# Last two experts' rows gathered, summed, normed and scattered; final norm of all rows moved behind expert 13

## The chip, the core and the metric

The kernel runs on one core of one Trainium2 chip. The time is that of one execution on the device, in microseconds (us). The engines are named as in the profile: PE does the matrix products, PEld loads their weights, DVE and ACT work on rows of elements and read the products' banks, POOL works on rows in SBUF only and issues the indirect transfers, SP issues the plain transfers.

## The reference, cut to what matters

One layer: norm and modulation, a mixer of two kinds of heads, then a mixture of 16 experts in which each expert chooses 128 of the 1,024 rows, and a last norm over every row. Only the end matters here:

```python
aff = softmax(einsum('bnd,de->bne', u, router_w))
gate, idx = lax.top_k(swapaxes(aff, 1, 2), 128)        # 128 rows for each expert
xs = u[idx]                                            # rows gathered
h = silu(xs @ w_gate) * (xs @ w_up)                    # 128 x 1024 by 1024 x 1024, per expert
y = (h @ w_down) * gate[..., None]
x = x + g2 * zeros(1024, 1024).at[idx].add(y)          # a row can be chosen by several experts
return x * rsqrt(mean(x * x, -1) + eps) * final_norm_w # all 1,024 rows
```

## The kernel before, in words

Everything up to the router's choice of rows is left alone by the change. It leaves in device memory `d_v` (the rows that experts read) and `d_acc` (the residual rows, 1,024 x 1,024, to which experts add), and in SBUF `idx` and `gate`, one column of 128 entries for each expert.

The loop over experts (L1330) then takes 16 turns. In turn e PE forms the gate product and the up product of expert e and the down product of expert e - 1 (`prod`, `down`), each of 8 weight tiles of 128 x 1,024. A weight tile is loaded by SP (`raw_load`), split by ACT into a rounded part and by DVE into the remainder (`split_w`, L922 and L923, DVE subtracting one SBUF tile from another), and multiplied in three passes of two products each. Four pairs of buffers hold split tiles; some 30 raw tiles in the list `free` let SP load far ahead, a freed tile being loaded again at once. `split_t` turns the rows of an expert by PE and splits them (`mh`, `ml` for the down product). After `down(e - 1)` POOL issues `scatter(e - 1)`: an indirect transfer that adds the 128 rows of `y` to `d_acc`. All engines take their instructions in the order of their own queue; the framework's scheduler writes that order, so a statement's place in the text is not its place in a queue.

The last two experts are not scattered. In turn 15 the kernel loads the last norm's weight (`fwb`), and builds one-hot matrices `ohs` (L1355) for the rows of experts 14 and 15. Behind the loop it loads all of `d_acc` as eight tiles of 128 rows (L1370), splits `y` of expert 14 and of expert 15 (L1373 and L1374, L1395 and L1396), and `rows_of` (L1383) multiplies the one-hot matrices by these, so that the rows of both experts arrive in a product bank in their places. `added` (L1406, L1407) adds them to the tile and takes the sum of squares; then come the root (L1414, and L1415 on POOL), the weight (L1418 on POOL, L1421 on DVE) and the scale (L1420 on ACT), and SP stores the tile (L1422). This chain of eight tiles starts when expert 15's down product (L1393) is done.

```python
        V.scalar_tensor_tensor(y[:, cs], po, gate[:, 15:16], g2b[j], op0=OP.mult, op1=OP.mult)
```

is the line (L1394) that yields half of expert 15's rows.

Of the kernel before, what the change touches and what calls it, by code (L numbers as in the profile page):

```python
# [9 lines left out]
F32 = mybir.dt.float32  # L10
# [9 lines left out]
P = 128  # L20
EPS = 1e-6
# [11 lines left out]
def tile_hybrid_block(ctx, tc, x, c, cx, c_ctx, ada_w, ada_b, norm1_w, w_in, conv_w, conv_b,  # L33
# [28 lines left out]
    def bank(tag, shape=(P, 512)):  # L62
        return psum.tile(list(shape), F32, name=tag, tag=tag, bufs={"mm": 4, "hg": 2, "ms": 2}[tag])
# [670 lines left out]
    srw, sorts = [tkr[:, 768:896], tkr[:, 896:1024], tk.tile([P, P], F32, name="srw")], []  # L734
    pos = const.tile([P, 8, 32], F32, name="lm", tag="lm", bufs=1)
    pay = tk.tile([P, 8, 16, 5], BF16, name="pay")
    last = tk.tile([P, 2], F32, name="last")
    slot = tk.tile([P, P], F32, name="slot")
    G.iota(slot, pattern=[[1, P]], base=-999, channel_multiplier=0, allow_small_or_imprecise_dtypes=True)
    same, low, other = (tk.tile([P, P], BF16, name=n) for n in ("same", "low", "other"))  # L740
# [166 lines left out]

    def take_r():

        raw = next(r for r in free if id(r) in tags)  # L910
        free.remove(raw)
        return tb(tags[id(raw)], [1024], 1, F32R)

    pairs = []

    def split_w():

        raw, (wh, wl) = raws.pop(0), pairs[0]
        pairs.append(pairs.pop(0))
        for i, r in enumerate(raw):  # L920
            cs = slice(1024 // len(raw) * i, 1024 // len(raw) * (i + 1))
            S.copy(wh[:, cs], r)  # L922
            V.tensor_sub(wl[:, cs], r, wh[:, cs])  # L923
        free.append(raw)
        raw_load()
        return wh, wl

    part = flat = lambda t: t.rearrange("p a b -> p (a b)")
# [325 lines left out]
    def pick(e):  # L1254

        oh = blk.tile([P, 8, P], BF16, name="mkt", tag="mkt", bufs=2)
        with tc.issue_after(found[-1].ins):
            V.tensor_tensor(oh, slot.unsqueeze(1).to_broadcast([P, 8, P]), pos[:, :, e:e + 1].to_broadcast([P, 8, P]), op=OP.is_equal)
        ps = bank("ms")
        for t in range(8):  # L1260
            T.matmul(ps[:, 0:5], oh[:, t, :], pay[:, t, e, :], start=(t == 0), stop=(t == 7))
        got = tb("got", [5], 2)
        S.copy(got, ps[:, 0:5])
        found.append(V.tensor_add(idx[:, e:e + 1], got[:, 3:4], got[:, 4:5]))
        if e > 13:
# [63 lines left out]
    gather(1)  # L1329
    for e in range(16):  # L1330
        pg, pu = [bank("mm"), bank("mm")], [bank("mm"), bank("mm")]
        prod(xh, xl, pg)
        if e < 14:
            pick(e + 2)
        prod(xh, xl, pu)
        if e == 0:
            hh, hl = (tb(n, [8, P], 1, F32R) for n in ("mh", "ml"))
            hb, y = (part(tb("go", [8, P], 2)) for _ in range(2))
            for j in range(2):
                g2b.append(part(tl("hsum", [4, P], 2)))  # L1340
                load(g2b[j], bass.AP(tensor=d_g.tensor, offset=d_g[3].offset + 512 * j, ap=[[0, P], [1, 512]]))
        if e < 15:
            split_t(xg, xh, xl)
        if e < 14:
            gather(e + 2)
        if e == 15:
            fwb = take(2)
            for j in range(2):
                load(fwb[j], bass.AP(tensor=final_w.tensor, offset=final_w.offset + 512 * j, ap=[[0, P], [1, 512]]))
            toks = take(2)[0]  # L1350
            G.iota(toks, pattern=[[1, 512]], base=0, channel_multiplier=0, allow_small_or_imprecise_dtypes=True)
            ohs = [take_r() for _ in range(2)]
            for i in range(2):
                for h in range(2):
                    V.tensor_scalar(ohs[i][:, 512 * h:512 * h + 512], toks, last[:, i:i + 1], -512.0 * h, op0=OP.subtract, op1=OP.is_equal)  # L1355
# [15 lines left out]
    ys = [[part(tb(n, [8, P], 1, F32R)) for n in ("xT", "mix")]]
    ys += [[[r[:, 512 * j:512 * j + 512] for j in range(2)] for r in (take_r(), take_r())]]
    S.copy(ys[0][0], y)  # L1373
    G.tensor_sub(ys[0][1], y, ys[0][0])  # L1374
    sq = tb("sq", [2, 8])
    sums = {}

    def rows_of(j, t):

        sums[j, t] = pb = bank("ms" if j else "mm")  # L1380
        for i in range(4):
            r = ys[i // 2][i % 2]
            T.matmul(pb, ohs[i // 2][:, t * P:(t + 1) * P], r[j] if i > 1 else r[:, 512 * j:512 * j + 512], start=(i == 0), stop=(i == 3))  # L1383

    for j in range(2):
        cs = slice(512 * j, 512 * j + 512)
        po = bank("hg")
        for q in range(4):
            wh, wl = weight()
            for k in (2 * q, 2 * q + 1):  # L1390
                fs_ = slice(512 * (k % 2), 512 * (k % 2) + 512)
                for p_, (l, r) in enumerate(((hh, wh), (hl, wh), (hh, wl))):
                    T.matmul(po, l[:, k, :], r[:, fs_], start=(k == 0 and p_ == 0), stop=(k == 7 and p_ == 2))  # L1393
        V.scalar_tensor_tensor(y[:, cs], po, gate[:, 15:16], g2b[j], op0=OP.mult, op1=OP.mult)  # L1394
        S.copy(ys[1][0][j], y[:, cs])  # L1395
        V.tensor_sub(ys[1][1][j], y[:, cs], ys[1][0][j])  # L1396
        if j == 0:
            for t in range(4):
                rows_of(0, t)
    def added(t):  # L1400
        if t > 3:
            rows_of(0, t)
        rows_of(1, t)
        for j in range(2):
            a = accs[t][:, 512 * j:512 * j + 512]
            V.tensor_add(a, a, sums[j, t])  # L1406
            S.activation(hb[:, 512 * j:512 * j + 512], a, AF.Square, scale=1.0 / 32, accum_out=sq[:, j, t:t + 1])  # L1407

    for t in range(9):
        if t < 8:  # L1410
            added(t)
        if t:
            a, r = accs[t - 1], tb("fr", [1], 4)
            V.tensor_scalar(r, sq[:, 0, t - 1:t], sq[:, 1, t - 1:t], EPS, op0=OP.add, op1=OP.add)  # L1414
            pw = G.tensor_tensor(r, r, mhalf[:, :1], op=OP.pow)  # L1415
        if t < 8:
            with tc.issue_after(pw.ins) if t > 5 else ExitStack():
                G.tensor_mul(accs[t][:, 0:512], accs[t][:, 0:512], fwb[0])  # L1418
        if t:
            S.mul(a[:, 0:512], a[:, 0:512], r)  # L1420
            V.scalar_tensor_tensor(a[:, 512:], a[:, 512:], r, fwb[1], op0=OP.mult, op1=OP.mult)  # L1421
            load(out[(t - 1) * P:t * P], a)  # L1422
# [27 lines left out]
```

## Time and profile before

| | us |
|---|---|
| three runs, median (lowest, highest) | 1563.09 (1559.11, 1565.22) |
| the profiled execution's own time | 1559.33 |
| its span in the trace | 1557.6 |

Times in the trace run from the start of the span. Of the 1.7 us between the profiled execution's time and its span the trace shows nothing. PE's clock was granted in full in most of the span; the mean is 0.967.

### The profile page before, as it was taken

The numbers are of one execution on the slowest core, as the hardware profiler recorded it, in microseconds if no ns is written. First come the engines' busy times: TensorE is split into PE (matmuls) and PEld (weight loads), VectorE is DVE, ScalarE is ACT, GpSimd is POOL, SyncE is SP. The second block draws the span as 40 slices with busy tenths as digits, with TensorE's granted clock in tenths as the row PEclk, the third lists the DMA queues.
The fourth block names the chain that finished last, engine by engine and source line by source line (L and its number), as shares of the span: only waits on it lengthen the run. The fifth ranks groups of instructions, "written<-read, shape, count | busy, mean of one in ns | idle before, by whom it ended". The sixth has DMA issues, their size and how long they took to land.

```text
span 1557.6 us, 23134 instructions
## 1 busy us (share of the span) xinstructions
PE 1447.8 (93%) x8121; PEld 1206.9 (77%) x8121; DVE 1230.4 (79%) x2193; ACT 864.7 (56%) x1454; POOL 174.8 (11%) x136
## 2 busy tenths in 40 slices
PE   7999999999999998988888947999999999999996
PEld 2899878888898896977677735888888888888764
DVE  3685577888866859546757796999999999998887
ACT  3764424334434343345545315777787787777775
POOL 0000000000002221210222110010000000000003
PEclk9999999999999998989898977999999999999998
DMA  9741311220334254276753486999999999999942
GB/s 268 258 128 31 110 54 35 75 82 22 115 102 142 82 149 149 72 194 211 223 183 112 158 320 211 370 391 374 386 387 384 385 389 383 387 376 362 352 141 109
DMA packets 181201, 337.31 MB, mean 217 GB/s; under 512 B 13560, under 2 KB 108348, under 8 KB 181084
## 3 DMA queue, kind: packets, MB, share of 16 engines
q1 hardware_dynamic: 176472, 319.99, 58.0%
q0 software_dynamic: 4320, 15.73, 4.1%
q8 instruction: 64, 1.05, 0.3%
q14 instruction: 53, 0.43, 0.1%
q10 hardware_dynamic: 292, 0.10, 0.0%
HBM read 303.38 MB, written 32.39 MB: 216 GB/s over the span
## 4 chain that ended last, share of the span: by engine, by line
PE 64%; DVE 13%; DMA 10%; issue 6%; ACT 4%; POOL 2%; SPq 0%; ACTq 0%; POOLq 0%; DVEq 0%
PE mm L1303 22%; PE mm L278 11%; PE hg L1303 10%; PE mm L286 5%; PE hg L350 3%; DMA MB<-d_nm 3%; DVE cacc L827 3%; PE hg L215 2%; PE ms L1288 2%; DMA wraw<-in_w_in_dram 1%; PE mm L1026 1%; PE ms L382 1%; POOL cacc L825 1%; DMA wraw<-in_ada_w_dram 1%; PE mm L496 1%
## 5 line engine op out<-in xcount | busy, mean ns | idle before, releaser
L286 PE MATMUL mm<-whi,uh 128*128 128x256 f32 (+1 forms) x512 | 145.6, 284 | 3.0 <-DVE Sb L386 1.3
L286 PE MATMUL mm<-wlo,uh 128*128 128x256 f32 (+1 forms) x512 | 145.1, 283 | 0.0
L286 PE MATMUL mm<-whi,ul 128*128 128x256 f32 (+1 forms) x512 | 144.8, 283 | 0.0
L253 DVE TENSOR_TENSOR wlo<-wraw,whi 128x512 fp32r<-128x512 f32 x96 | 64.7, 686 | 49.5 <-ACT whi L252 49.0
L286 PEld LDWEIGHTS mm<-whi,uh 128*128 128x128 f32 x512 | 96.7, 189 | 5.2 <-DVE Sb L386 1.5
L286 PEld LDWEIGHTS mm<-whi,ul 128*128 128x128 f32 x512 | 96.8, 189 | 0.0
L286 PEld LDWEIGHTS mm<-wlo,uh 128*128 128x128 f32 x512 | 96.3, 188 | 0.3
L1303 PE MATMUL mm<-qkx,xT 128*128 128x512 f32 x256 | 83.7, 408 | 0.6 <-ACT xT L1289 0.3
L827 DVE SCALAR_TENSOR_TENSOR cacc<-pad,cols,cacc 128x1024 f32<-128x1024 f32 x48 | 63.6, 1325 | 24.4 <-POOL cacc L825 23.6
L1303 PE MATMUL mm<-E,xT 128*128 128x512 f32 x256 | 81.2, 398 | 0.4 <-ACT E L922 0.4
L1303 PE MATMUL mm<-MB,xT 128*128 128x512 f32 x256 | 80.8, 397 | 0.0
L252 ACT CAST whi<-wraw 128x512 fp32r<-128x512 f32 x96 | 58.4, 620 | 38.3 <-PE mm L278 24.8
L344 ACT COPY hgc<-hgK 128x512 f32<-128x512 f32 x56 | 35.5, 634 | 78.1 <-DVE hgK L363 38.6
L350 PE MATMUL hg<-hgQ,hgc 128*128 128x128 f32 x448 | 65.9, 291 | 1.0 <-DVE hgQ L366 1.0
L350 PEld LDWEIGHTS hg<-hgQ,hgc 128*128 128x128 f32 x448 | 57.8, 191 | 10.8 <-issue 6.9
L278 PE MATMUL mm<-uh,whi 128*128 128x512 f32 x192 | 63.4, 405 | 0.0
L278 PE MATMUL mm<-ul,whi 128*128 128x512 f32 x192 | 63.4, 404 | 0.0
L278 PE MATMUL mm<-uh,wlo 128*128 128x512 f32 x192 | 61.5, 399 | 0.0
L297 DVE SCALAR_TENSOR_TENSOR ac<-wraw,csil,ac 128x256 f32<-128x256 f32 x112 | 55.9, 499 | 4.1 <-DMA wraw<-in_ada_w_dram 2.2
L1303 PEld LDWEIGHTS mm<-E,xT 128*128 128x128 f32 x256 | 47.9, 189 | 13.7 <-ACT E L922 1.7
L1303 PEld LDWEIGHTS mm<-MB,xT 128*128 128x128 f32 x256 | 48.2, 188 | 11.9
L359 DVE COPY_PREDICATED hgA<-lm,hg 128x512 f32<-128x512 uint8 x56 | 41.4, 740 | 18.4 <-PE hg L350 17.1
(602 smaller groups left out, 4304.2 us busy)
## 6 DMA issues: line engine op xcount, KB each, us to landing
wraw<-in_w_in_dram SPq DMA_DIRECT2D x48, 512.0 KB
wl<-in_exp_w_up_dram SPq DMA_DIRECT2D x34, 512.0 KB
wh<-in_exp_w_up_dram SPq DMA_DIRECT2D x34, 512.0 KB
wh<-in_exp_w_gate_dram SPq DMA_DIRECT2D x34, 512.0 KB
wl<-in_exp_w_gate_dram SPq DMA_DIRECT2D x34, 512.0 KB
wraw<-in_ada_w_dram SPq DMA_DIRECT2D x32, 512.0 KB
wl<-in_exp_w_down_dram SPq DMA_DIRECT2D x29, 512.0 KB
wh<-in_exp_w_down_dram SPq DMA_DIRECT2D x29, 512.0 KB
```

The lines of the kernel that those rows point to most:

```text
L215: T.matmul(pm[0:2, :256], csil[:, k, :], adas[i, k // 4][:, k % 4, :, :], start=(k == 0), stop=(k == 7))
L252: S.copy(hi[:, :, cs], src)
L253: V.tensor_sub(lo[:, :, cs], src, hi[:, :, cs])
L278: T.matmul(o, l, r[:, k, i * n:(i + 1) * n], start=(k == 0 and q == 0), stop=(k == 7 and q == 2))
L286: T.matmul(o, l[:, k, ts], r, start=(k == 0 and q == 0), stop=(k == 7 and q == 2))
L297: V.scalar_tensor_tensor(ac, a2[:, k % 4, :], csil[:, k, 0:1], ac, op0=OP.mult, op1=OP.add)
L344: S.copy(view(kc, 0, [[h, 2], [2 * h, 256 // h], [1, h]]), view(K, 0, [[512 + h, 2], [2 * h, 256 // h], [1, h]]))
L350: T.matmul(pb[:, cc, :], kc[:, cc * P:(cc + 1) * P], view(Q, cc * P, pat), start=True, stop=True)
L359: V.copy_predicated(A, lmask[h].unsqueeze(1).to_broadcast([P, 4, P]), scores(h))
L827: V.scalar_tensor_tensor(acc, tap(t), tapw(t, r), acc, op0=OP.mult, op1=OP.add)
L1288: T.transpose(pt[:, k, :], view(src, 4 * q + k, [[8, P]]), ident)
L1303: T.matmul(o, l[:, k, :], r[:, 512 * j:512 * j + 512], start=(k == 0 and p_ == 0), stop=(k == 7 and p_ == 2))
```

## The change

With e the turn: in turn 14, right after `scatter(13)`, `norm_start` asks for a first tile of `d_acc`, a gather of expert 14's 128 rows of `d_acc` into `rows_[14]`, the norm's weight as one 128 x 1,024 tile and a second tile of `d_acc`. From there `weight` advances the generator `norms` at every third call. Each step norms one tile of 128 rows as if no expert were still to come: the sum of squares on ACT, then on POOL a product with the weight, a sum, a power and a product with the root, and a store by SP two steps later. Thus all 1,024 rows are normed and stored without experts 14 and 15.

`row_out` then repairs the 256 rows of these two: DVE adds `y` to the gathered rows, ACT squares, POOL takes the root, DVE forms the normed rows, and POOL scatters them over `out`. Rows of expert 14 are also scattered back to `d_acc`, from which expert 15's rows are then gathered, since a row can belong to both. A scatter over `out` waits for every store before it (`add_manual_dep`). So that tiles are free for all this, ten freed raw tiles are not loaded again (`hold`). The one-hot matrices, their products, the splits of `y` and the chain behind expert 15 go.

```diff
@@ split_w
         free.append(raw)
-        raw_load()
+        if hold and len(raw) == 1:
+            hold.pop()
+        else:
+            raw_load()
@@ weight
+        if accs:
+            fin["n"] = fin.get("n", 0) + 1
+            if fin["n"] > 3 and fin["n"] % 3 == 1:
+                next(dense, None)
@@ new functions
+    def acc_rows(e):
+        rows_[e] = take(1)
+        G.indirect_dma_start(out=rows_[e], out_offset=None, in_=d_acc,
+                             in_offset=bass.IndirectOffsetOnAxis(ap=idx[:, e:e + 1], axis=0))
+    def norms():
+        for t in range(10):
+            if t > 1:
+                stored.append(load(out[(t - 2) * P:(t - 1) * P], accs[t - 2]))
+            if t + 2 < 8:
+                acc_load(t + 2)
+            if t < 8:
+                a, r = accs[t], sq[:, t:t + 1]
+                S.activation(fin["junk"], a, AF.Square, scale=1.0 / 32, accum_out=r)
+                G.tensor_mul(a, a, fin["w"])
+                G.tensor_scalar(r, r, EPS, None, op0=OP.add)
+                G.tensor_tensor(r, r, mhalf[:, :1], op=OP.pow)
+                G.tensor_mul(a, a, r.to_broadcast([P, 1024]))
+            yield
+    def row_out(e, js):
...
+            V.tensor_add(rows_[e][:, cs], rows_[e][:, cs], y[:, cs])
+            S.activation(y[:, cs], rows_[e][:, cs], AF.Square, scale=1.0 / 32, accum_out=sq[:, 8 + 2 * i + j:9 + 2 * i + j])
...
+        if e == 14:
+            G.indirect_dma_start(out=d_acc, out_offset=..., in_=rows_[14], in_offset=None)
+        r, o = tb("fr", [1], 2), hb if e == 15 else fin["junk"]
+        V.tensor_scalar(r, ..., EPS, op0=OP.add, op1=OP.add)
+        G.tensor_tensor(r, r, mhalf[:, :1], op=OP.pow)
+        V.scalar_tensor_tensor(o, rows_[e], r, fin["w"], op0=OP.mult, op1=OP.mult)
+        d = G.indirect_dma_start(out=out, out_offset=..., in_=o, in_offset=None)
+        for s_ in stored:
+            tc.add_manual_dep(d.ins, s_.ins.name, DATA, reason="rows stored again")
+        stored.append(d)
@@ the loop over experts
+        if e == 14:
+            hold.extend(range(10))
...
-        if e == 15:
-            fwb = take(2)
...
-                    V.tensor_scalar(ohs[i][:, 512 * h:512 * h + 512], toks, last[:, i:i + 1], -512.0 * h, ...)
...
+        if e == 14:
+            norm_start()
+        if e == 15:
+            for _ in dense:
+                pass
+            row_out(14, (0, 1))
+            acc_rows(15)
@@ behind the loop
-    accs = []
-    for i in range(8):
-        accs.append(take(1))
-        load(accs[i], d_acc[P * i:P * i + P])
...
-            T.matmul(pb, ohs[i // 2][:, t * P:(t + 1) * P], ...)
...
         V.scalar_tensor_tensor(y[:, cs], po, gate[:, 15:16], g2b[j], op0=OP.mult, op1=OP.mult)
-        S.copy(ys[1][0][j], y[:, cs])
-        V.tensor_sub(ys[1][1][j], y[:, cs], ys[1][0][j])
...
+        row_out(15, (j,))
```

What the scheduler makes of it shows in the queues. ACT, from the middle of expert 14's down product (L922 before, L921 now, is the split of a weight tile; the second cast of `mh` must wait until that down product has used up the first contents). Before:

```order
L922 CAST qkx<-xm 128x1024
L1289 CAST mh<-ms 128x512
L922 CAST E<-S_8976 128x1024
L922 CAST MB<-kin 128x512 x2
L922 CAST v_8613<-tkr 128x1024
L922 CAST qkx<-v_7887 128x1024
L1289 CAST mh<-ms 128x512
```

Now (L1355 is a norm's sum of squares):

```order
L921 CAST qkx<-xm 128x1024
L1289 CAST mh<-ms 128x512
L1355 ACTIVATE v_8346,sq<-S_8976 128x1024
L1355 ACTIVATE v_8346,sq<-wor 128x1024
L921 CAST E<-kin 128x512 x2
L921 CAST MB<-wor 128x1024
L921 CAST v_8612<-wor 128x1024
L1355 ACTIVATE v_8346,sq<-v_7416 128x1024
L1289 CAST mh<-ms 128x512
```

The first two squares stand between the first cast of `mh` and the casts of the last three weight tiles of expert 14's down product; no norm stands further ahead.

POOL, from the scatter of expert 13 on. Before, a few instructions between that scatter and the chain behind expert 15:

```order
L1314 DMA d_acc<-go,idx 1024x1024 x2
L1351 IOTA wh_8751 128x512
L1374 TENSOR_TENSOR mix<-go,xT 128x1024
L1418 TENSOR_TENSOR wl_8754<-wl_8754,Sb 128x512
L1418 TENSOR_TENSOR wh_8755<-wh_8755,Sb 128x512
```

Now (`S_8976`, `wor` and so on are the tiles of `d_acc`, L1356 the product with the weight, L1357 the sum with eps, L1358 the power, L1359 the product with the root):

```order
L1318 DMA d_acc<-go,idx 1024x1024 x2
L1333 DMA tkr<-d_acc,idx 128x1024
L1357 TENSOR_SCALAR sq<-sq 128x1
L1358 TENSOR_TENSOR sq<-sq,mhalf 128x1
L1356 TENSOR_TENSOR S_8976<-S_8976,v_7886 128x1024
L1359 TENSOR_TENSOR S_8976<-S_8976,sq 128x1024
L1356 TENSOR_TENSOR wor<-wor,v_7886 128x1024
L1357 TENSOR_SCALAR sq<-sq 128x1
L1358 TENSOR_TENSOR sq<-sq,mhalf 128x1
L1359 TENSOR_TENSOR wor<-wor,sq 128x1024
```

All eight tiles run through POOL with four instructions each.

POOL's end, before and then now:

```order
L1415 TENSOR_TENSOR fr<-fr,mhalf 128x1 x5
L1418 TENSOR_TENSOR wl_8760<-wl_8760,Sb 128x512
L1415 TENSOR_TENSOR fr<-fr,mhalf 128x1
L1418 TENSOR_TENSOR wh_8761<-wh_8761,Sb 128x512
L1415 TENSOR_TENSOR fr<-fr,mhalf 128x1
```

```order
L1374 DMA d_acc<-tkr,idx 1024x1024
L1356 TENSOR_TENSOR wor<-wor,v_7886 128x1024
L1357 TENSOR_SCALAR sq<-sq 128x1
L1358 TENSOR_TENSOR sq<-sq,mhalf 128x1
L1359 TENSOR_TENSOR wor<-wor,sq 128x1024
L1333 DMA wl_8759<-d_acc,idx 128x1024
L1379 DMA out_dram<-v_8346,idx 1024x1024
L1377 TENSOR_TENSOR fr<-fr,mhalf 128x1
L1379 DMA out_dram<-go,idx 1024x1024
```

The gather of expert 15's rows (the second L1333) and both scatters over `out` (L1379) stand behind the last of the eight tiles; the scatter of expert 14's rows to `d_acc` (L1374) stands ahead of the eighth.

## Rows read from the trace of the kernel before

**Rows 1.** The page's first part: busy us, share of the span and number of instructions of each engine.

```profile
PE 1447.8 (93%) x8121; PEld 1206.9 (77%) x8121; DVE 1230.4 (79%) x2193; ACT 864.7 (56%) x1454; POOL 174.8 (11%) x136
```

**Rows 2.** The view of stretches, at the end of the span: start and end, length, then busy us and instructions of PE, PEld, DVE, ACT and POOL, then the granted clock of PE, the DMA share and GB/s.

```profile
1500.00:1510.00 10.00, 9.70 (x44) 7.18 (x43) 8.59 (x10) 4.91 (x7) 0.00 (x0) 1.00 1.00 374
1510.00:1520.00 10.00, 6.72 (x27) 4.58 (x26) 8.95 (x9) 6.61 (x8) 2.61 (x1) 1.00 0.18 72
...
1530.00:1540.00 10.00, 10.00 (x45) 7.93 (x43) 7.00 (x12) 5.78 (x16) 7.25 (x7) 1.00 0.00 1
1540.00:1550.00 10.00, 3.95 (x14) 2.21 (x13) 9.56 (x18) 7.50 (x18) 3.98 (x6) 0.98 0.65 262
1550.00:1558.00 8.00, 0.00 (x0) 0.00 (x0) 2.62 (x3) 2.03 (x4) 2.33 (x3) 0.50 0.48 197
```

**Rows 3.** The chain of work that ended last, in order of time: start us, us, engine, what it wrote, line.

```profile
1527.92 4.20 PE hg L1393 x18
...
1536.70 0.92 PE ms L1383 x4
...
1553.22 0.75 DVE wh L1421
```

**Rows 4.** Instructions in order of time on ACT, in expert 14's down product: start us, us, engine, line, operation, out<-in, shapes, and in brackets the idle time before and what ended it.

```profile
1506.82 0.59 ACT L1289 CAST mh<-ms 128x512 fp32r<-128x512 f32 x1 [3.95 <-PE hg L1303]
1507.30 1.05 ACT L922 CAST E<-S 128x1024 fp32r<-128x1024 f32 x1
```

**Rows 5.** Groups of instructions on POOL by line and shape: line, engine, operation, out<-in, shapes, count | busy us, mean ns of one | idle us before and what ended it.

```profile
L1314 POOL DMA_INDIRECT d_acc<-go,idx x14 | 22.4, 1601 | 191.9 <-DVE go L1311 191.9
L1055 POOL TENSOR_TENSOR vt<-vt,B2b 128x1024 f32<-128x1024 f32 x8 | 19.0, 2373 | 16.3 <-DVE vt L1054 11.5 <-DVE den L979 4.8
L946 POOL TENSOR_TENSOR MB<-MB,mu_b 128x1024 f32<-128x1024 f32 x8 | 17.7, 2208 | 84.5 <-ACT E L943 77.0 <-PE ms L1011 7.5
L155 POOL TENSOR_TENSOR r<-r,mhalf 128x4 f32<-128x4 f32 x8 | 8.2, 1027 | 44.5 <-DVE r L154 39.2 <-DVE mx L1066 5.3
L1415 POOL TENSOR_TENSOR fr<-fr,mhalf 128x1 f32<-128x1 f32 x8 | 4.4, 552 | 7.7 <-DVE fr L1414 7.7
L1437 POOL MEMSET const-float32-1.0<- 128x1 f32 x1 | 0.1, 95 | 0.0
```

**Rows 6.** Instructions in order of time (columns as in rows 4) at three places where POOL and DVE work at once.

```profile
1515.80 2.61 POOL L1374 TENSOR_TENSOR mix<-go,xT 128x1024 fp32r<-128x1024 f32 x1 [35.99 <-ACT xT L1373]
1516.05 3.43 DVE L923 TENSOR_TENSOR qkx<-v,E 128x1024 fp32r<-128x1024 f32 x1
...
1535.75 0.68 DVE L1406 TENSOR_TENSOR wh<-wh,ms 128x512 f32<-128x512 f32 x1
1535.77 1.30 POOL L1418 TENSOR_TENSOR wl<-wl,Sb 128x512 f32<-128x512 f32 x1
...
1550.56 1.26 POOL L1418 TENSOR_TENSOR wh<-wh,Sb 128x512 f32<-128x512 f32 x1
1550.63 1.75 DVE L1421 SCALAR_TENSOR_TENSOR wl<-wl,fr,Sb 128x512 f32<-128x512 f32 x1 [0.73 <-POOL fr L1415]
```

**Rows 7.** The same view in an earlier stage (a convolution), where POOL has two instructions in a row; neighbours of one kind are merged, with their sum.

```profile
506.26 5.71 POOL L825 TENSOR_TENSOR cacc<-cacc,cone 128x1024 f32<-128x1024 f32 x2 [5.10 <-ACT cone L824]
506.83 2.88 DVE L267 TENSOR_TENSOR vlo<-wraw,vhi 128x512 fp32r<-128x512 f32 x1
509.64 4.73 DVE L827 SCALAR_TENSOR_TENSOR cacc<-pad,cols,cacc 128x1024 f32<-128x1024 f32 x2
```

**Rows 8.** Durations by line and tile: line, engine, operation, out<-in, count, ns shortest/median/longest, first and last start us, shapes.

```profile
L923 DVE TENSOR_TENSOR E<-wh,MB x25: 1210/1217/1226, 961.1 to 1524.6; 128x1024 fp32r<-128x1024 f32 x25
L923 DVE TENSOR_TENSOR qkx<-kin,E x6: 679/684/685, 996.1 to 1364.6; 128x512 fp32r<-128x512 f32 x6
L1394 DVE SCALAR_TENSOR_TENSOR go<-hg,gate,hsum x2: 741/746/750, 1523.9 to 1532.2; 128x512 f32<-128x512 f32 x2
L1054 DVE SCALAR_TENSOR_TENSOR vt<-xm,r,A2b x8: 1273/1284/1285, 743.0 to 912.9; 128x1024 f32<-128x1024 f32 x8
L1052 ACT ACTIVATE vt<-xm x8: 1040/1057/1060, 738.4 to 910.6; 128x1024 f32<-128x1024 f32 x8
L1052 ACT ACTIVATION_READ_ACCUMULATOR vt<-xm x8: 185/186/193, 739.4 to 911.6; 128x1 f32 x8
```

**Rows 9.** Time from an indirect transfer's issue to its landing, first of the gathers of an expert's rows from `d_v`, then of the scatters that add to `d_acc`.

```profile
DMA to landing us min/median/max: 4.5/6.5/7.8
DMA to landing us min/median/max: 6.1/7.7/9.2
```

**Rows 10.** Issues of transfers in order of time: the last load of expert 14's down weights that keeps its place, the last weight load of all, expert 13's scatter, and the last store.

```profile
1459.20 0.33 SPq L892 DMA_DIRECT2D xm<-in_exp_w_down_dram  x1
...
1475.69 0.37 SPq L897 DMA_DIRECT2D wl<-in_exp_w_down_dram  x1
...
1477.64 1.57 POOL L1314 DMA_INDIRECT d_acc<-go,idx  x1 [36.35 <-DVE go L1311]
...
1554.04 0.33 SPq L1422 DMA_DIRECT2D out_dram<-wh  x1
```

**Rows 11.** The view of stretches (columns as in rows 2), in a stage where PE works little more than half of the time.

```profile
680.00:690.00 10.00, 5.95 (x30) 5.71 (x29) 4.98 (x14) 7.95 (x19) 3.90 (x2) 0.67 0.77 195
```

More of the change, by code (lines that the diff above doesn't have):

```diff
@@ L736, in tile_hybrid_block @@
     pay = tk.tile([P, 8, 16, 5], BF16, name="pay")
-    last = tk.tile([P, 2], F32, name="last")
     slot = tk.tile([P, P], F32, name="slot")
@@ L912, in take_r @@
         return tb(tags[id(raw)], [1024], 1, F32R)
-    pairs = []
+    pairs, hold = [], []
     def split_w():
@@ L1264, in pick @@
         found.append(V.tensor_add(idx[:, e:e + 1], got[:, 3:4], got[:, 4:5]))
-        if e > 13:
-            V.tensor_add(last[:, e - 14:e - 13], got[:, 3:4], got[:, 4:5])
         V.tensor_reduce(gate[:, e:e + 1], got[:, 0:3], axis=AX.X, op=OP.add)
@@ L1319, in gather, with acc_load @@
                              in_offset=bass.IndirectOffsetOnAxis(ap=idx[:, e:e + 1], axis=0))
+    accs, rows_, fin, stored = [], {}, {}, []
+    sq = tb("sq", [12])
+    DATA = mybir.DependencyInfo(mybir.DependencyClass.Sync, mybir.DependencyReason.DATA)
+    def acc_rows(e):
+        rows_[e] = take(1)
+        G.indirect_dma_start(out=rows_[e], out_offset=None, in_=d_acc,
+                             in_offset=bass.IndirectOffsetOnAxis(ap=idx[:, e:e + 1], axis=0))
+    def acc_load(t):
+        accs.append(take(1) if t < 6 else accs[t - 6])
+        load(accs[t], d_acc[P * t:P * t + P])
@@ new lines, in norm_start @@
+    def norm_start():
+        acc_load(0)
+        acc_rows(14)
+        fin["w"], fin["junk"] = take(1), take(1)
+        load(fin["w"], bass.AP(tensor=final_w.tensor, offset=final_w.offset, ap=[[0, P], [1, 1024]]))
+        acc_load(1)
+    def norms():
[12 more added lines that the diff above has]
+            yield
@@ new lines, in tile_hybrid_block @@
+    dense = norms()
+    def row_out(e, js):
+        i = e - 14
+        for j in js:
+            cs = slice(512 * j, 512 * j + 512)
+            V.tensor_add(rows_[e][:, cs], rows_[e][:, cs], y[:, cs])
+            S.activation(y[:, cs], rows_[e][:, cs], AF.Square, scale=1.0 / 32, accum_out=sq[:, 8 + 2 * i + j:9 + 2 * i + j])
+        if js[-1] == 0:
+            return
+        if e == 14:
+            G.indirect_dma_start(out=d_acc, out_offset=bass.IndirectOffsetOnAxis(ap=idx[:, 14:15], axis=0), in_=rows_[14], in_offset=None)
+        r, o = tb("fr", [1], 2), hb if e == 15 else fin["junk"]
+        V.tensor_scalar(r, sq[:, 8 + 2 * i:9 + 2 * i], sq[:, 9 + 2 * i:10 + 2 * i], EPS, op0=OP.add, op1=OP.add)
+        G.tensor_tensor(r, r, mhalf[:, :1], op=OP.pow)
+        V.scalar_tensor_tensor(o, rows_[e], r, fin["w"], op0=OP.mult, op1=OP.mult)
+        d = G.indirect_dma_start(out=out, out_offset=bass.IndirectOffsetOnAxis(ap=idx[:, e:e + 1], axis=0), in_=o, in_offset=None)
+        for s_ in stored:
+            tc.add_manual_dep(d.ins, s_.ins.name, DATA, reason="rows stored again")
+        stored.append(d)
@@ L1345, in tile_hybrid_block @@
             gather(e + 2)
-        if e == 15:
-            fwb = take(2)
[L1348 to L1355, printed above, removed]
         for j in range(2):
@@ L1363, in tile_hybrid_block @@
                 scatter(e - 1)
-        split_t(hb, hh, hl)
-    accs = []
-    for i in range(8):
-        accs.append(take(1))
-        load(accs[i], d_acc[P * i:P * i + P])
[L1371 to L1383, printed above, removed]
+        if e == 14:
[5 more added lines that the diff above has]
+            acc_rows(15)
+        split_t(hb, hh, hl)
     for j in range(2):
-        cs = slice(512 * j, 512 * j + 512)
         po = bank("hg")
@@ L1393, in tile_hybrid_block @@
                     T.matmul(po, l[:, k, :], r[:, fs_], start=(k == 0 and p_ == 0), stop=(k == 7 and p_ == 2))
+        cs = slice(512 * j, 512 * j + 512)
         V.scalar_tensor_tensor(y[:, cs], po, gate[:, 15:16], g2b[j], op0=OP.mult, op1=OP.mult)
-        S.copy(ys[1][0][j], y[:, cs])
-        V.tensor_sub(ys[1][1][j], y[:, cs], ys[1][0][j])
[L1397 to L1422, printed above, removed]
+        row_out(15, (j,))
 _INS = ['x', 'c', 'ctx', 'c_ctx', 'ada_w', 'ada_b', 'norm1_w', 'w_in', 'conv_w', 'conv_b', 'hg_lb_logits', 'ml_gate_b',
```

## The prediction

> **What bounds the kernel now.** I read the page's first part, then the view of stretches over the end, then the chain that ended last, and last the instructions in order of time on POOL, DVE and ACT. POOL is busy for 11% of the span [rows 1], so work moved to it looks free. The stretches show the end that the change goes for: PE is full until 1540, then fades, and nothing of it runs after 1550 [rows 2]. On the chain, expert 15's down product ends at 1532.1 (1527.92 + 4.20), the one-hot products at 1537.6, and one more tile after another follows until DVE's last 0.75 us at 1553.22; a last store is issued at 1554.04 and the span ends at 1557.6 [rows 3, 10]. So 25.5 us lie behind expert 15. The change takes most of this away and puts other work in its place, on POOL.
>
> **When POOL can begin.** The tile of `d_acc` waits for expert 13's scatter, issued at 1477.64 and landed 6.1 to 9.2 us later, by 1487 at most [rows 9, 10]. It is not that which decides. The first square stands on ACT behind the first cast of `mh`, and that cast waited 3.95 us for PE and ended at 1507.4 [rows 4]. Nothing ahead of it changes, so I keep the time. The square takes 1.06 + 0.19 us [rows 8]: POOL begins at about 1508.7, not at 1487. SP, in contrast, stands still from the load at 1459.20 until that scatter has landed, with the last 11 weight loads behind it; the last two also wait for the first tile's store. I count nothing for this: the loads had been issued by 1475.69 [rows 10], the first of them is split at 1507.3 [rows 4], and after 1487 some 20 us are left. If this cover were gone, PE would lose time, not POOL.
>
> **POOL's own work.** Eight products with the weight at 2.37 us (128 x 1024, two inputs, the row of L1055): 19.0. Eight products with the root, whose second input is a repeated element as in L946, at 2.21: 17.7. Nine powers on one column at 0.55: 5.0 [rows 5]. Eight sums on one column have no row; a fill of one column (0.10) is the lower bound and a power on four columns (1.03) the upper; I take 0.5, by the power on one column, which has the same shape: 4.0 (0.8 to 8.2). One issue of a scatter at 1.6 [rows 5]. Sum: **47.3 us** (44.1 to 51.5). Undisturbed, POOL's last tile would be normed at 1556.0, 24 us after PE's last product of today.
>
> **What it does to DVE, and DVE to it.** DVE's split of a weight tile takes 1.22 us [rows 8]. The one at 1516.05, started beside a POOL product of 2.61, took 3.43: it ended 1.07 us after POOL, as if it had begun there. L1421 took 1.75 beside POOL and 0.75 without it [rows 3, 6]. L1406, with one input in a product bank, stayed at 0.68 beside a POOL product [rows 6]. So instructions with both inputs in SBUF take turns with POOL, others don't mind. Turns go both ways: in the convolution POOL's two took 5.71 and not twice 2.4, while DVE's 0.68 and 1.28 became 2.88 and 3.45 (4.73 less 1.28) [rows 6, 7]. Between 1508.7 and the end of the products DVE has these: the two half tiles at 0.68 and two tiles at 1.22 that are left of expert 14's down weights, eight tiles of expert 15's at 1.22, two sums of `row_out` at 0.68, one 128 x 1024 product at 1.28 [rows 8]. That is 1.4 + 2.4 + 9.8 + 1.4 + 1.3 = **16.3 us**, and POOL, which always has a next instruction, waits for nearly all of it. Hence POOL's eighth tile is done at 1508.7 + 47.3 + 16.3 = **1572.3**.
>
> PE is late too, but under this. ACT's two squares hold the next casts back by 2.5 us. Then 14 DVE instructions (15.0 us of the 16.3) each wait for a POOL instruction, of mean 47.3 / 34 = 1.4 us: 15.0 + 19.5 from 1510, and some 4 for `y` and `mh`, ends expert 15's product at about 1549 instead of 1532. Its clock could fall in such gaps: with PE busy for 5.95 of 10 us the granted clock was 0.67 [rows 11]. At 1.2 GHz the six matmuls of a tile take 2.8 instead of 1.4 us (18 in 4.20 [rows 3]); for 11 tiles that is 15 us more at worst, 1564, still ahead of POOL. I count nothing for it.
>
> **Behind POOL's last tile (X).** Two paths follow. SP stores the eighth tile: at most 3.6 us, as the last store today (1554.04 to 1557.6) [rows 10]. Only then may expert 14's scatter over `out` be issued; it lands after 6.1, and expert 15's after it lands 6.1 later, by the shortest of the scatters that add. I take the shortest, since those rows were read beside weight loads and here no loads run; a scatter that doesn't add has no row (the gathers' 4.5 is the nearer bound below, the scatters' 9.2 above) [rows 9]. That is X + 15.8. The other path, the gather at 4.5 [rows 9], two sums, a square, a power and a product (1.36 + 1.25 + 0.55 + 1.28 [rows 5, 8]), is ready at X + 8.9, before expert 14's scatter has landed at X + 9.7, and so costs nothing. The end: 1572.3 + 15.8 = 1588.1 in the span, and with the 1.7 us around it 1589.8 against 1559.3 of the same execution: **about 30 us slower**. The removed work (64 one-hot matmuls, the splits, the chain) is in this sum already, since the end is built anew from 1508.7. The median of the three runs lies 3.8 above the profiled execution; I leave the forecast at 1590 and let the range reach for that.
>
> A rule weighed against this: the Trainium skill, DMA: Bandwidth & Descriptors, section "Anatomy of one DMA — SWDGE (gpsimd) path", gives such a transfer about 2.0 us plus its bytes at 436 GB/s, an estimate of 3.2 us for 512 KB. Rows 9 show 4.5 at the least, under load; by the page the sum would end near 1584, by the rows at 1590.
>
> **The rivals.**
> *Short landings.* With the queues empty, indirect transfers may land like the plain store, in 3.6 us [rows 10]. Then the gather's path leads: 3.6 + 4.4 = X + 8.0, and a scatter's 3.6 ends at X + 11.6 = 1583.9, 1585.6 with what lies around. For it speaks that all rows 9 stem from a loaded stretch; against it, that no indirect transfer came under 4.5. The page named above gives the same direction.
> *POOL is not held up.* If DVE waits for POOL but seldom the other way round, X is 1556.0 and the time 1556.0 + 15.8 + 1.7 = 1573.5. Rows 7 speak against it.
> *The norms stay hidden: faster.* Were POOL ready before expert 15's rows, only these would follow 1532.1: 0.75 for `y`, 0.68, 1.25, 0.55, 1.28 and a scatter of 6.1, that is 1542.7 and with 1.7 more 1544, 15 us faster. It decides at ACT's queue: 47 us of POOL before about 1536 need a first square by 1487, when the scatter has just landed. As the queue stands, the square is behind a cast that PE frees at 1506.8.
> *Cheap products.* If the products on POOL took half as long as L1055, X would be near 1551 and the time near 1568, hardly over the bound for slower. All rows of 128 x 1024 on POOL speak against it.
>
> **How the numbers follow.** Forecast 0.55, short landings 0.18, POOL not held up 0.15, hidden norms 0.05, the rest (cheap products, splits that fill the gaps better) 0.07. The range runs from 1572, just under the third case, to 1604: X later by 4 (sums at 1.03), landings at the median (7.7 twice: 3.2), some 0.07 us of handing over at 34 instructions (2.4), and the 3.8 of the median. It leaves out the hidden norms, the rest, and less than a tenth above. Half a per cent (8 us) is about what a measurement of this kernel can tell from no change. Faster by more: 0.05; within: 0.05; slower: 0.90.
>
> **What would show it.** In the changed profile: POOL busy from about 1509 to past 1565, with 16 instructions of 2.2 to 2.4 us; L922's remainders in the last 11 tiles at 1.3 to 3.6 us instead of 1.22; PE busy for less than half of 1510 to 1550, expert 15's product ending near 1549; on the chain's end POOL's products, the eighth tile's store, then two scatters one after the other. The forecast is wrong if squares run before 1500, if POOL's products beside DVE's splits don't lengthen those, or if the chain's end is PE and `row_out` with POOL already idle.

## The result and the profile after

On the same chip the kernel before took 1561.10 us (median of 4 runs) and the changed kernel 1582.36 us (1580.74 to 1585.05, 4 runs): ratio 1.0135, 95% interval 1.0106 to 1.0165. The profiled execution took 1582.9 us, its span is 1581.1, 23.5 longer than before's 1557.6; the forecast was 1590, with a span of 1588.1. The whole last stretch starts some us earlier or later from one profile to the next (expert 13's scatter, which the change leaves alone, is issued at 1477.64 before [rows 10] and at 1479.71 now), so below I measure the ends from that scatter: by it the end comes 21.4 us later. For the changed kernel, L922 is now the remainder of a weight tile, L1436 expert 15's down product and L1438 its `y`.

First the page's part 1: busy us, share of the span and instructions of each engine [rows 1].

```profile
PE 1436.2 (91%) x8057; PEld 1194.2 (76%) x8057; DVE 1225.2 (77%) x2161; ACT 857.6 (54%) x1435; POOL 217.0 (14%) x157
```

The totals hardly speak: PE lost 11.6 us of work and POOL gained 42.2. The stretches [rows 2] do (columns: start and end, length, busy us of PE, PEld, DVE, ACT and POOL, granted clock, DMA share, GB/s):

```profile
1500.00:1510.00 10.00, 10.00 (x48) 7.86 (x46) 7.59 (x10) 4.24 (x5) 0.00 (x0) 1.00 0.93 348
1510.00:1520.00 10.00, 5.12 (x12) 2.45 (x10) 7.96 (x5) 5.67 (x10) 9.13 (x6) 0.68 0.30 93
1520.00:1530.00 10.00, 5.67 (x13) 3.75 (x14) 7.69 (x10) 6.00 (x11) 9.61 (x7) 0.67 0.66 223
1530.00:1540.00 10.00, 8.84 (x29) 5.99 (x27) 9.84 (x6) 7.55 (x10) 9.77 (x7) 0.80 0.31 106
1540.00:1550.00 10.00, 4.27 (x16) 2.85 (x16) 7.10 (x5) 1.57 (x4) 9.77 (x5) 1.00 0.44 157
1550.00:1560.00 10.00, 0.00 (x0) 0.00 (x0) 0.00 (x0) 0.00 (x0) 9.37 (x9) 0.55 0.15 59
1560.00:1570.00 10.00, 0.00 (x0) 0.00 (x0) 0.00 (x0) 0.00 (x0) 7.25 (x7) 0.50 0.56 201
1570.00:1581.00 11.00, 0.00 (x0) 0.00 (x0) 2.79 (x4) 1.33 (x4) 1.70 (x3) 0.50 0.25 98
```

POOL is full from 1510 on and alone from 1550, and PE is thinner than before from 1510 on, where POOL starts (5.12 against 6.72 us in the first ten, 8.84 against 10.00 from 1530 to 1540 [rows 2]). Next POOL in order of time: its start, the second tile, the last tile and the end (start us, us, line, operation, out<-in, idle before and what ended it).

```profile
1510.64 0.24 POOL L1357 TENSOR_SCALAR sq<-sq 128x1 f32<-128x1 f32 x1 [20.64 <-ACT v L1355]
...
1516.15 2.80 POOL L1356 TENSOR_TENSOR wor<-wor,v 128x1024 f32<-128x1024 f32 x1
1519.03 1.10 POOL L1357 TENSOR_SCALAR sq<-sq 128x1 f32<-128x1 f32 x1
1520.21 1.40 POOL L1358 TENSOR_TENSOR sq<-sq,mhalf 128x1 f32<-128x1 f32 x1
1521.69 1.89 POOL L1359 TENSOR_TENSOR wor<-wor,sq 128x1024 f32<-128x1024 f32 x1
...
1560.27 2.35 POOL L1356 TENSOR_TENSOR wor<-wor,v 128x1024 f32<-128x1024 f32 x1
1562.69 0.23 POOL L1357 TENSOR_SCALAR sq<-sq 128x1 f32<-128x1 f32 x1
1563.00 0.57 POOL L1358 TENSOR_TENSOR sq<-sq,mhalf 128x1 f32<-128x1 f32 x1
1563.64 1.89 POOL L1359 TENSOR_TENSOR wor<-wor,sq 128x1024 f32<-128x1024 f32 x1
1565.70 1.10 POOL L1333 DMA_INDIRECT wl<-d_acc,idx  x1 [0.17 <-issue]
1569.12 0.99 POOL L1379 DMA_INDIRECT out_dram<-v,idx  x1 [2.33 <-DMA out_dram<-wor]
1573.26 0.57 POOL L1377 TENSOR_TENSOR fr<-fr,mhalf 128x1 f32<-128x1 f32 x1 [3.14 <-DVE fr L1376]
1575.44 1.02 POOL L1379 DMA_INDIRECT out_dram<-go,idx  x1 [1.61 <-DVE go L1378]
```

The last tile is what POOL's four instructions cost alone (DVE stands still then); the second is the same four beside DVE. DVE in the same stretch, three lengthened remainders and one that was not, and at the end its wait for the gather:

```profile
1516.66 3.38 DVE L922 TENSOR_TENSOR E<-wor,MB 128x1024 fp32r<-128x1024 f32 x1
1519.97 1.21 DVE L922 TENSOR_TENSOR mlc<-wor,v 128x1024 fp32r<-128x1024 f32 x1
...
1532.68 3.41 DVE L922 TENSOR_TENSOR mlc<-wh,v 128x1024 fp32r<-128x1024 f32 x1
...
1540.62 3.40 DVE L922 TENSOR_TENSOR E<-wh,MB 128x1024 fp32r<-128x1024 f32 x1
...
1570.87 1.29 DVE L1369 TENSOR_TENSOR wl<-wl,go 128x512 f32<-128x512 f32 x2 [22.20 <-DMA wl<-d_acc,idx]
```

The remainder at 1516.66 began behind POOL's product of 1516.15 and ended 1.09 us after it, as the one in [rows 6] did. Then it is the other way round: the remainder at 1519.97 takes its plain 1.21, and POOL's power at 1520.21 takes 1.40 instead of 0.57. ACT shows that the start of it all stayed where it was [rows 4]: the first cast of `mh` behind PE, the first square behind that.

```profile
1508.91 0.59 ACT L1289 CAST mh<-ms 128x512 fp32r<-128x512 f32 x1 [3.96 <-PE hg L1307]
1509.39 1.06 ACT L1355 ACTIVATE v<-S 128x1024 f32<-128x1024 f32 x1
```

The chain of work that ended last, from the eighth tile's product with the root on (start us, us, what) [rows 3]:

```profile
1563.65 1.89 POOL wor L1359
1565.56 2.64 DMA out_dram<-wor
...
1569.12 0.99 POOL out_dram L1379
1570.12 3.10 issue
```

It is drawn through POOL, the eighth tile's store and expert 14's scatter; the 3.10 us are POOL waiting for expert 15's rows, whose gather was issued at 1565.70. So behind the eighth tile it is the gather's path that decides, not that store. Last, the indirect transfers of the end, with us from issue to landing [rows 9]:

```profile
d_acc<-tkr,idx POOLq DMA_INDIRECT x1, 3.9
wl<-d_acc,idx POOLq DMA_INDIRECT x1, 5.1
out_dram<-v,idx POOLq DMA_INDIRECT x1, 3.4
out_dram<-go,idx POOLq DMA_INDIRECT x1, 3.4
```

### The profile page after: what moved, and what is told of

It reads as the page before. It is cut to its first block, busy times and chain, and to the rows that moved or that the text cites. A ratio compares the mean times of both kernels' runs of the same rounds, so it can differ in the third digit from the quotient of the medians.

```text
span 1581.1 us, 22968 instructions
## 1 busy us (share of the span) xinstructions
PE 1436.2 (91%) x8057; PEld 1194.2 (76%) x8057; DVE 1225.2 (77%) x2161; ACT 857.6 (54%) x1435; POOL 217.0 (14%) x157
## 4 chain that ended last, share of the span: by engine, by line
PE 63%; DVE 11%; DMA 9%; issue 6%; POOL 6%; ACT 4%; SPq 0%; POOLq 0%; ACTq 0%; DVEq 0%
PE mm L1307 21%; PE mm L278 10%; PE hg L1307 10%; PE mm L286 6%; PE hg L350 3%; DMA MB<-d_nm 3%; DVE cacc L826 2%; PE hg L215 2%; PE ms L1288 2%; DMA wraw<-in_w_in_dram 1%; PE ms L382 1%; POOL cacc L824 1%; PE mm L1028 1%; PE mm L496 1%; ACT E L945 1%
## 5 line engine op out<-in xcount | busy, mean ns | idle before, releaser
L253 DVE TENSOR_TENSOR wlo<-wraw,whi 128x512 fp32r<-128x512 f32 x96 | 64.8, 688 | 49.8 <-ACT whi L252 49.2
L1322 POOL DMA_INDIRECT vt<-d_v,idx x16 | 16.3, 1017 | 332.7 <-PE ms L1288 253.0
L824 POOL TENSOR_TENSOR cacc<-cacc,cone 128x1024 f32<-128x1024 f32 x16 | 39.3, 2453 | 132.7 <-ACT cone L823 132.0
```

What stands on the lines that cost most here:

```text
L253: V.tensor_sub(lo[:, :, cs], src, hi[:, :, cs])
L824: G.tensor_add(acc, acc, one)
```

## The experiments

In this table both ends are counted from the issue of expert 13's scatter in the same profile (1477.64 before [rows 10], 1479.71 after, then 1474.51, 1475.27, 1477.15, 1479.50, 1473.59, 1474.58, 1476.17), which takes out when the stretch began. Each kernel has one profile. "Product" is the end of expert 15's last down matmul, "end" that of the span.

| kernel | product, us | end, us | time, us | ratio to before (95%) |
|---|---|---|---|---|
| before | 54.5 | 80.0 | | 1 |
| after | 67.0 | 101.4 | 1582.36 | 1.0135 (1.0106 to 1.0165) |
| e1_fill | 54.6 | 94.7 | 1573.22 | 1.0109 (1.0076 to 1.0142) |
| e2_no_weight | 59.0 | 82.3 | 1561.5 | 1.0034 (1.0018 to 1.0050) |
| e3_products_dve | 60.9 | 82.1 | 1561.2 | 1.0026 (1.0012 to 1.0041) |
| e4_five_tiles | 67.0 | 90.9 | 1569.98 | 1.0083 (1.0058 to 1.0108) |
| e5_early_gather | 64.8 | 75.2 | 1553.3 | 0.9977 (0.9963 to 0.9990) |
| e6_early_gather_spread | 60.2 | 76.3 | 1554.17 | 0.9989 (0.9977 to 1.0001) |
| e7_gather_first | 60.8 | 72.3 | 1551.17 | 0.9956 (0.9938 to 0.9973) |

The kernel before ran in each comparison of an experiment, with medians of 1556 to 1557 us; beside the changed kernel it had 1561.10. So the ratios can be compared from line to line, the times only roughly. e1, e2 and e4 leave out work of the kernel, as told in their expectations; e3, e5, e6 and e7 compute all of it.

**e1_fill**: POOL's two products of each tile become fills of about the same length, which read nothing.

```diff
-                G.tensor_mul(a, a, fin["w"])
+                for z in (a, a, a[:, 0:512]): G.memset(z, 0.0)
...
-                G.tensor_mul(a, a, r.to_broadcast([P, 1024]))
+                for z in (a, a): G.memset(z, 0.0)
```

> The kernel after the change, with each of POOL's sixteen 128 x 1024 products put in by fills of the same tile of about the same length (three fills of 1024, 1024 and 512 columns for the product with the weight, two of 1024 for the product with the root; about 0.95 us per 1024). It leaves out the norm of the rows that experts 14 and 15 did not choose. A fill reads nothing from SBUF. Theory (POOL's queue sets the end, and takes turns with DVE where both read SBUF): DVE's remainders of the last eleven weight tiles go back to about 1.22 us, expert 15's product ends near 1537 instead of 1546.7 in the span, POOL's eight tiles take about 47 us instead of 54.9 because its waits for DVE go, and the time falls by about 7 to 1575 us. Rival (PE is late for the squares on ACT and the late loads, not for POOL; any work of POOL hinders DVE): the remainders stay long, expert 15's product still ends near 1546, and the time is that of the change or a few us more, 1582 to 1586.

Measured: POOL busy from 1505.42 to 1554.33, 48.9 us against 54.9 before the edit, yet no remainder of a whole tile on DVE above 1.23 us, and the product is at 54.6 instead of 67.0. POOL's one-column instructions still waited. Of DVE and POOL, between 1524 and 1528:

```profile
1524.94 1.22 DVE L922 TENSOR_TENSOR E<-wh,MB 128x1024 fp32r<-128x1024 f32 x1
1526.08 1.22 DVE L922 TENSOR_TENSOR mlc<-wl,v 128x1024 fp32r<-128x1024 f32 x1
```

```profile
1525.16 0.96 POOL L1356 MEMSET wl<- 128x1024 f32 x1
1526.09 1.64 POOL L1358 TENSOR_TENSOR sq<-sq,mhalf 128x1 f32<-128x1 f32 x1
```

So the 12.4 us by which PE's product moved hang on POOL's products, which read SBUF; POOL being busy with fills costs DVE nothing. From the scatter to the product PE's same 194 matmuls are busy for 48.5 us instead of 53.8, at a mean granted clock of 0.97 instead of 0.87, and PE idles for 7.1 us less: part of the delay was the clock that fell while PE was thinned out. That the kernel before has nearly the same 54.5 does not mean that nothing else delays PE in e1_fill, since before the change 3.0 us of one-hot products (L1383) lay on the chain ahead of that product. The end gained only 6.7 us (7 expected): POOL's eighth tile was done 79.8 us behind the scatter instead of 85.8. The Trainium skill (SBUF — State Buffer, "Who interferes with whom") says that a VectorE instruction with two SBUF inputs contends with a GpSimd instruction that reads SBUF and not with one that only writes; the trace agrees, 1.22 beside fills of 0.96 and 3.4 beside products.

**e2_no_weight**: one product less.

```diff
-                G.tensor_mul(a, a, fin["w"])
```

> The kernel after the change without POOL's product with the norm's weight (eight instructions of 2.35 us); the weight is left out of the rows that experts 14 and 15 did not choose. Theory (POOL's queue sets the end): its own work falls from 42 to 23 us, the eighth tile is normed near 1546 instead of 1565.5, the gather of expert 15's rows then waits for expert 14's scatter to land (about 1547.5), and the same 15.6 us follow: about 1564 us. Rival (the serial indirect transfers and the lateness of PE set the end, POOL beside them): 1580 to 1582.

Measured: the end moves by 19.1 us (101.4 to 82.3), the eight products' own 8 x 2.36 = 18.9. The end goes with the length of POOL's queue. That it moves by their own time and no more is in part chance: POOL's eight tiles still take some 12.8 us more than their own work, but 3.1 of these are now a wait for the sum behind expert 14's squares.

**e4_five_tiles**: both products only for the first five tiles (`if t < 5`).

> The kernel after the change with both of POOL's products left out for the last three of the eight tiles (the norm's scale and weight are left out of 384 rows). In the changed kernel these six products run when DVE and PE are done. Theory (POOL's queue sets the end up to its last tile): PE and DVE are as before up to 1547, the six products' 13 us go, but the gather of expert 15's rows must then wait for expert 14's scatter to land, so that 3 of them come back: about 1572 us. Rival (what counts is the turn-taking up to 1547 and the transfers behind it; POOL's last tiles lie beside them): 1580 to 1582.

Measured: the product stays at 67.0, since the first five tiles are those that meet it, and the end moves by 10.5. The three tiles' products are worth 3 x (2.36 + 1.89 + some 0.1) = 13; some of it went into a wait of POOL, 3.14, for expert 14's scatter to `d_acc`, behind which the gather stands. PE's delay alone thus costs nothing in the changed kernel; POOL sets the end.

**e3_products_dve**: both products in one instruction on DVE; POOL keeps sum and power.

```diff
-                G.tensor_mul(a, a, fin["w"])
...
-                G.tensor_mul(a, a, r.to_broadcast([P, 1024]))
+                V.scalar_tensor_tensor(a, a, r, fin["w"], op0=OP.mult, op1=OP.mult)
```

> The kernel after the change with POOL's two products per tile made by one instruction of DVE (a scalar-tensor-tensor product of 1.28 us); sum, power, loads, squares, gathers and scatters stay as they are. All of the reference is computed. Theory (the 20 us come from the products on POOL): POOL has only short instructions, expert 15's product ends near 1538, DVE has 5 us of products behind it, and the time is near 1556 us, some 5 below the kernel before. Rival (other parts of the change cost the 20 us: the loads that wait for expert 13's scatter, the squares ahead of casts on ACT, the scatters one after the other): above 1570 us.

Measured: 5 us above what was expected, and 4 above the kernel before where 5 below it was expected; 19.3 of the 21.4 us that the end had lost come back, and no more. Why, POOL's rows show:

```profile
1536.69 0.57 POOL L1358 TENSOR_TENSOR sq<-sq,mhalf 128x1 f32<-128x1 f32 x1
1537.59 1.09 POOL L1374 DMA_INDIRECT d_acc<-tkr,idx  x1 [0.34 <-issue]
...
1541.29 2.09 POOL L1333 DMA_INDIRECT wl<-d_acc,idx  x1 [0.85 <-DMA d_acc<-tkr,idx]
1549.43 0.99 POOL L1379 DMA_INDIRECT out_dram<-v,idx  x1 [6.05 <-DVE wl L1369]
...
1553.60 1.02 POOL L1379 DMA_INDIRECT out_dram<-go,idx  x1 [2.56 <-DMA out_dram<-v,idx]
```

Expert 14's rows had been summed at 1522.2, but their scatter stands on POOL behind seven tiles' sums and powers, which wait for ACT's squares. Scatter, gather and sum follow one another from 1537.59 on, while PE's product ended at 1538.0.

**e5_early_gather** and **e6_early_gather_spread** draw that conclusion: the row sum of expert 14, its scatter and the gather come right behind the product of expert 14, all tiles of `d_acc` have buffers of their own, and each tile's square and product stand behind one weight's cast.

```diff
         if e == 15:
-            for _ in dense:
-                pass
-            row_out(14, (0, 1))
+            row_add(14, (0, 1))
+            G.indirect_dma_start(out=d_acc, out_offset=..., in_=rows_[14], in_offset=None)
             acc_rows(15)
```

> Complete computation, norm products on VectorE as in e3_products_dve, and in addition: all eight row tiles loaded at once behind expert 13's scatter (each in a buffer of its own), the scatter of expert 14's rows and the gather of expert 15's issued on POOL as soon as expert 14's rows are summed and not behind tile 6, the tiles' squares and products each put behind one weight's cast. Theory (in e3_products_dve the end hung on POOL's queue: scatter 1537.6, gather 1541.3, while PE was done at 1538): the end now follows PE's last product: 1538 + some 5 for the sum, square, power and product of expert 15's rows + 5.6 from the issue of the last scatter to the end of the span = 1549, with 1.7 around it some 1550, ratio to before 0.992 to 0.998. Rival (VectorE's and ScalarE's 20 us of norms and the eight loads ahead of the last weights hold PE up instead): PE's last product ends at 1545 or later and the time is 1557 or more, ratio 1.000 or above.

> As e5_early_gather, but the row tiles from the third on are loaded between the last weights (one behind every second weight) and not at once. Theory: if the eight loads in a row delayed the last weights in e5_early_gather, this is faster than it by up to some 4 us, and the gather of expert 15's rows comes later since the scatter of expert 14's rows must follow the last tile's load. Rival: the weights were early enough, and this is no faster than e5_early_gather, or slower by what the later gather costs (0 to 6 us).

Measured: e5 is 0.23% below before, within the ratio that was expected. That its span is the expected one (1548.8 against 1549) is luck: the sum took over e3's end of PE at 1538, but e5's stretch began 3.6 us earlier, and counted from the scatter the product came at 64.8 and not at 60.9; the median, 1553.3, is 3 above what was expected. In e5 POOL and DVE show what held PE:

```profile
1518.21 1.90 POOL L1358 TENSOR_SCALAR sq<-sq 128x1 f32<-128x1 f32 x1
1520.19 2.59 POOL L1359 TENSOR_TENSOR sq<-sq,mhalf 128x1 f32<-128x1 f32 x1
1522.96 2.12 POOL L1335 DMA_INDIRECT wl<-d_acc,idx  x1 [0.18 <-issue]
```

```profile
1524.68 1.22 DVE L922 TENSOR_TENSOR MB<-wl,qkx 128x1024 fp32r<-128x1024 f32 x1
1529.46 0.69 DVE L1372 TENSOR_TENSOR wl<-wl,go 128x512 f32<-128x512 f32 x1 [3.56 <-DMA wl<-d_acc,idx]
```

Two POOL instructions on one column took 4.5 us instead of 0.8, beside DVE instructions that followed each other without a gap; the gather came late for that, and a row sum that waited for it stood on DVE ahead of three weights.

In e6 PE's product comes 4.6 us earlier, but the end 1.1 us later: no faster than e5, as the rival said. The gather is issued at 1531.02 instead of 1522.96 (7.1 us later, counted from the scatter), but the row sum waited only 0.29 us for it. What came behind PE's product took 10.6 us up to the last scatter's issue instead of 4.8, for the order of the queues:

```profile
1537.00 1.29 DVE L1373 TENSOR_TENSOR wl<-wl,go 128x512 f32<-128x512 f32 x2 [0.29 <-DMA wl<-d_acc,idx]
```

```profile
1539.38 0.55 POOL L1381 TENSOR_TENSOR fr<-fr,mhalf 128x1 f32<-128x1 f32 x1 [5.39 <-DVE fr L1380]
1540.41 1.75 POOL L1383 DMA_INDIRECT out_dram<-tkr,idx  x1 [0.47 <-issue]
1545.29 0.95 POOL L1383 DMA_INDIRECT out_dram<-go,idx  x1 [3.14 <-DMA out_dram<-tkr,idx]
```

Both halves of expert 15's rows are summed behind PE, and expert 14's scatter, whose rows were ready at 1536.7, stands on POOL behind expert 15's power, so that expert 15's scatter waits 3.14 us for its landing. PE's gain is not shown to come from the loads: e7_gather_first loads all tiles at once, as e5 does, and has it nearly whole (60.8).

**e7_gather_first** turns round both orders that held e5, and puts each tile's product one weight later.

```diff
-                G.tensor_scalar(r, r, EPS, None, op0=OP.add)
+                with tc.issue_after(fin["g"][t > 3].ins):
+                    G.tensor_scalar(r, r, EPS, None, op0=OP.add)
...
-        row_add(15, (j,))
+    row_add(15, (0, 1))
     row_out(15)
```

> Complete computation, as e5_early_gather but for two orders: on POOL the gather of expert 15's rows stands ahead of the sums and powers of tiles 4 to 7 (there it stood behind two of them, which took 1.9 and 2.6 us each beside VectorE, and came at 1522.96, 9.0 us behind the scatter that it follows); on VectorE both halves of expert 15's row sum stand behind the last weight's remainder (there the first half stood ahead of the last three weights' and made them wait 3.56 us for that gather), and each tile's product is put one weight later. Theory: PE's last product ends some 3 us earlier (1535 to 1536 where scatter(13) is issued at 1473.6), and the span some 3 us earlier too: 1545 to 1547, time 1547 to 1550, ratio to before 0.993 to 0.997. Rival (PE waits for something else there, such as ScalarE's squares, and the 3.56 us were beside it): PE ends near 1538 as before, ratio 0.997 to 0.999.

Measured: the product comes 4.0 us earlier than in e5 and the end 2.9 (3 expected); the time, 1551.17, is 1 us above the expected band, the ratio within it (in the profiled execution, of 1550.27 us, the stretch began 2.6 us later than in e5's). That it is faster than e5 is shown by the two profiles alone: the intervals of the ratios overlap. POOL's end:

```profile
1538.46 1.11 POOL L1383 DMA_INDIRECT out_dram<-tkr,idx  x1 [1.61 <-DVE tkr L1382]
1540.65 0.57 POOL L1381 TENSOR_TENSOR fr<-fr,mhalf 128x1 f32<-128x1 f32 x1 [1.08 <-DVE fr L1380]
1542.83 1.04 POOL L1383 DMA_INDIRECT out_dram<-go,idx  x1 [1.61 <-DVE go L1382]
```

From PE's last matmul (1536.97) to the last scatter's issue are 5.9 us (4.8 in e5, hence 2.9 and not 4.0 at the end), and on POOL only expert 14's scatter and one power lie in between. This version is 0.44% faster than the kernel before (0.27 to 0.62%), so the idea of the change pays a little once its products are not POOL's and the short steps stand early in the queues.

## Why the prediction held, and where it was off

The mechanism was right: POOL's queue sets the end, DVE and PE are slowed on the way without counting. Of the list of signs, POOL's start (1510.6) came, and the chain's end is POOL's. Lengthened remainders came in six of the last 11 tiles (2.65 to 3.41, two half tiles together 4.48); the other five stayed at 1.21. Not seen were products of 2.2 to 2.4 us throughout (they took 1.89 alone and up to 3.37 beside DVE), PE busy for less than half of 1510 to 1550 (23.9 of 40 us), nor the second scatter following the first one's landing. The late weight loads cost nothing, as counted: no cast of ACT from 1500 on waited for one. The forecast span was 7.0 us too long, step by step:

- **POOL's begin**: 1508.7 forecast, 1510.64 measured. It stood behind `mh` as said; the 1.9 us are the 2.07 by which the whole stretch ran later.
- **POOL's own work**: 47.3 forecast; by the rows of undisturbed instructions 8 x 2.36 + 8 x 1.89 + 9 x 0.57 + 8 x 0.23 + 1.1 = 42.1. Mis-sized were the product with the root (1.89, not L946's 2.21, a saving of 2.6), the sums (0.23, not 0.5, 2.2) and the scatter's issue (0.5). L946's mean in [rows 5] is one of two groups: in the trace of before three of its eight took 1.89 or 1.90, five 2.35 to 2.43.
- **Turns with DVE**: 16.3 forecast; POOL took 54.9 from 1510.64 to the end of its eighth tile at 1565.53, so 12.8 over its own work: 11.1 of lengthened instructions and 1.7 of handing over, which the sum had left out. POOL did not wait for every DVE instruction: beside the remainder at 1516.66 POOL's product had begun first, and it was DVE that waited. Summed over the rows, DVE lost 13.7 us (19.5 forecast). e1_fill shows that this is a matter of POOL reading SBUF, and that 12.4 us of PE's delay hang on it.
- **PE's product**: 17 us later forecast, 12.5 measured. The granted clock was 0.68 and 0.67 in the mean of the two stretches in which PE was busy for 5.12 and 5.67 of 10 us; from 1514 to 1522 and from 1528 to 1534 it was 0.50, the lower level of 1.2 GHz (PE had been busy for 0.27 of the 2 us from 1510, and for 0.73 of the 4 us from 1524). The forecast counted nothing for it, and nothing reached the end: e4_five_tiles, with the product still at 67.0 and the end 10.5 earlier, confirms that PE's delay lies under POOL.
- **Behind the eighth tile**: 15.8 forecast, 15.6 measured, but by the other path. The step "ready at X + 8.9, before expert 14's scatter has landed at X + 9.7, and so costs nothing" failed. Here X = 1565.5; expert 14's scatter was issued at X + 3.6 and landed 3.4 later, at X + 7.0, while the gather took 5.1 and expert 15's rows were ready at X + 9.6 and their scatter issued at X + 9.9, so these lead, as the rival *short landings* had it. That 15.8 and 15.6 agree is luck. The last scatter was issued at X + 9.9 where the sum had X + 9.7, for another reason; and from that issue to the span's end are 5.7, 3.4 to the landing and 2.2 more, which the sum had put at nothing, where it had 6.1 for the landing alone. The scatters of [rows 9] were the wrong neighbours: they add to their rows and ran beside weight loads. Of the load the runs show a part: scatters that don't add took 3.4 in e5 at a DMA share of 0.58 and 4.9 in e4 at 0.90. What adding costs no run shows. The Trainium skill's rule that was weighed there (DMA: Bandwidth & Descriptors, "Anatomy of one DMA — SWDGE (gpsimd) path", an estimate of 3.2 us) is near the scatters' 3.4 and far from the gather's 5.1.

The rival *POOL is not held up* (X at 1556.0) is refuted by the rows beside DVE, *cheap products* by 2.35 and 1.89 us alone. (The sum for that rival was some 3.5 us short: sixteen products at 1.19 us instead of 36.7 in all put X at 1554.6, not near 1551.) The hidden norms did not come about in the changed kernel, but e7_gather_first ends 11.5 us behind PE's product, close to that rival's sum of 10.6: what stood against it was POOL and the orders of the queues.

## What to carry to other kernels

An idle POOL is not free room beside a DVE that forms sums of two SBUF tiles: each POOL product costs its own time on POOL and, where the two meet, up to 2.2 us on DVE (3.41 instead of 1.21), so price both and put the work into one fused DVE instruction when DVE has gaps. When an engine's queue holds bulk work and a short step that others wait for (here a scatter and the gather behind it), read the order of that queue first; moving the step ahead of the bulk work brought 7 us between e3 and e5 (with the tiles' loads, squares and products moved too, so that the share of each is not shown). To compare ends of profiles whose upstream parts differ by some us, count from a common event.

## What the runs showed that was not expected

- POOL's instructions on one column, 0.23 and 0.57 us alone, took 1.90 and 2.59 in a row beside DVE instructions with two SBUF inputs (e5); in the changed kernel 1.10 and 1.40.
- A product with a repeated element took 1.89 us on POOL, one with two full tiles 2.35, at the same 128 x 1024.
- In the end, where no weights are loaded, indirect scatters of 128 rows landed after 3.4 to 3.9 us and the gather after 5.1; the gathers under load took 4.5 to 7.8 [rows 9].
- Issuing a gather kept POOL for 1.10 us with DVE still, and for 2.12 beside it (e5).
